# GpSimd passes in pieces of 256 columns, and one exponential per head for the decay matrix

## Chip, cores and metric

The kernel runs on one core of a Trainium2 chip. The metric is device time in microseconds (us) of one execution; the time before is the median of three runs.

## What is computed

One layer of an encoder over two requests (4096 and 2048 tokens of width 1024, that is 32 + 16 tiles of 128 tokens) with shared weights. The input is layer-normalised, projected, split among three mixers (windowed attention, a gated DeltaNet in both directions, attention over 256 memory tokens), gated, projected out, added to the input and normalised again. The parts that the change touches:

```python
def layer_norm(x, g, b):                      # on the input and on the memory tokens
    mu = xf.mean(-1, keepdims=True); var = jnp.square(xf - mu).mean(-1, keepdims=True)
    return (xf - mu) * lax.rsqrt(var + LN_EPS) * g + b
...
q = l2norm(heads(q)) * DN_KEY_DIM ** -0.5     # l2norm(t) = t * rsqrt(sum(t*t) + 1e-6)
k = l2norm(heads(k))
...
g = jnp.cumsum(g, axis=-1)
decay = exp(where(causal, g[..., :, None] - g[..., None, :], -inf))
k_beta = k * beta[..., None]
a = einsum('...id,...jd->...ij', k_beta, k) * decay      # then a triangular solve with a
qk = einsum('...id,...jd->...ij', q, k) * decay
```

The kernel works with the decay matrix multiplied by the step's beta, so each of its entries is the exponential of a sum: the row of cumulated gates of the one position, less the cumulated gate of the other, plus the logarithm of beta, plus a mask that is 0 or -30000.

## The kernel before

The work stands in three stages, each over the 48 tiles in pairs. Stage one (0 to about 1390 us) makes for each tile the input norm (`front`), the projections (`proj`), the short convolution and the normalised keys and queries of the DeltaNet (`conv`), and the windowed attention (`attention`). Stage two (about 1560 to 2450 us) runs the DeltaNet forward in time, with the gates' projections (`gate_proj`) and the memory attention (`memory`) beside it; stage three (2450 us to the end) runs it backward in time, with the output projection and the last norm (`finish`) beside it. Between stages one and two both overlap.

No line of the source is issued at once. `V`, `S`, `G`, `T` and `Q` (VectorE, ScalarE, GpSimd, TensorE and the DMA queue of SyncE) are recorders of the class `Plan`: each call is noted with its tiles and a cost from a table (for GpSimd 200 ns + 2.1 ns a column). When a pool closes, a list scheduler puts all noted operations of a stage in order, engine by engine, by those costs, the number of buffers of each tile and the latest time at which each operation is due; it makes seven orders and keeps the one that its own costs like best. Its costs know of no engine that holds up another. Then everything is issued in that order, and all engines work strictly in order. So all compute instructions have the one source line L505, and are told apart by tiles.

The places that the change touches:

- `front` (L819): for each of 48 input tiles and 4 tiles of memory tokens. VectorE takes the statistics (`bst`, `bmv`), GpSimd the power -1/2 (`brs`), ScalarE normalises `x` (128x1024, f32) in place, GpSimd multiplies `x` by the row `grow` and adds the row `brow`, each in one instruction over 1024 columns. Then `split` makes a high half (ScalarE) and a low half (VectorE, `xhl`), and a DMA transposes both to `xT`. `x` has three buffers, `xhl` one, `xT` two (of a pair each).
- `conv` (L1414): for each pair of tiles, per three blocks, a convolution of five taps: ScalarE the first, VectorE four `scalar_tensor_tensor` on `acc` for each of two halves. Then per tile GpSimd adds halves to `n32` (tile `n`), ScalarE squares, VectorE sums (`nss`) and adds an epsilon, GpSimd takes the power -1/2, VectorE multiplies by 1024, GpSimd multiplies `n32` by it (512 columns), and `split` makes `kqtm`.
- `gates` (L1362): six times, for eight tiles at once, the gates: `lnb` is the logarithm of beta, `ncum` the negative cumulated gate (a copy on ScalarE from PSUM).
- `dn_prep` (L869): for each tile and direction (96 times). `e` is the tile `cr` (128 x 4 heads x 128), loaded as a broadcast row. VectorE adds the mask; ScalarE adds `ncum` for each of four heads (Identity with a bias), then takes the exponential for each head with the bias `lnb`. VectorE multiplies the two products in PSUM (`psk`) with it, to `n` and `p`.
- `dn_invert`: for each four tiles a triangular inverse on GpSimd, 60 dependent instructions (`tb`, `nb`) after two DMAs.

Of the kernel before, what the change touches and what calls it, by code (L numbers as in the profile page):

```python
# [13 lines left out]
AF = mybir.ActivationFunctionType  # L14
ALU = mybir.AluOpType
# [4 lines left out]
P = 128  # L20
D = 1024
# [529 lines left out]
def encoder(ctx: ExitStack, tc: tile.TileContext, A, outs):  # L551
    nc = tc.nc
    plan = Plan(tc)
    V, S, G, T, Q = plan.engines()
# [12 lines left out]
    def ctile(shape, dt, name):  # L567
        return const.tile(shape, dt, name=name, tag=name)
# [7 lines left out]
    def sc1(name):  # L576
        nscal[0] += 1
        return scal[:, nscal[0] - 1:nscal[0]]
# [209 lines left out]
    ncum = ctile([P, 2, NT, 4], F32, "ncum")  # L788
    lnb = ctile([P, 2, NT, 4], F32, "lnb")
# [27 lines left out]
    grow_in, brow_in = grow, brow  # L817

    def front(pool, src_rows, xT_out, hl_dram=None, x_dram=None):  # L819

        x = gx.tile([P, D], F32, tag="x", name="x", bufs=3)
        Q.dma_start(out=x, in_=src_rows)
        rs, nb = layer_norm_stats(pool, x, LN_EPS, "f")
        S.activation(x, x, AF.Identity, scale=rs, bias=nb)
        G.tensor_tensor(x, x, grow_in, op=ALU.mult)
        G.tensor_tensor(x, x, brow_in, op=ALU.add)
        hl = pool.tile([P, 2, D], F16, tag="xhl", name="xhl", bufs=1)
        split(None, hl[:, 0, :], hl[:, 1, :], x)
        flat = hl.rearrange("p a b -> p (a b)")
        if xT_out is not None:  # L830
            Q.dma_start_transpose(out=xT_out, in_=flat)
        if hl_dram is not None:
            Q.dma_start(out=hl_dram, in_=flat)
        if x_dram is not None:
            Q.dma_start(out=x_dram, in_=x)
# [33 lines left out]
    def dn_prep(pool, psp, dr, t, e, n):  # L869

        fm = pool.tile([P, 8, P], F16, tag="fm", name="fm", bufs=2)
        Q.dma_start_transpose(out=fm, in_=dst_d[t].rearrange("p h t s d -> p (h t s d)"))

        ks = pool.tile([P, 4, P], F16, tag="ks", name="ks", bufs=KSB)
        kv = fm.rearrange("p (h t) m -> p h t m", t=2)[:, :, 1]
        for i in range(2):
            S.activation(ks[64 - 64 * i:128 - 64 * i], kv[64 * i:64 * i + 64], AF.Copy)
        lb = lnb[:, dr, t]
        nc_ = ncum[:, dr, t]
        d = {}  # L880

        V.tensor_tensor(e, e, dmask[dr][2].unsqueeze(1).to_broadcast([P, 4, P]), op=ALU.add)
        for h in range(4):
            S.activation(e[:, h], e[:, h], AF.Identity, bias=nc_[:, h:h + 1])
        for h in range(4):
            S.activation(e[:, h], e[:, h], AF.Exp, bias=lb[:, h:h + 1])
        d["eg"] = egs[:, :, dr, t]

        p = pool.tile([P, 4, P], F32, tag="p", name="p", bufs=1)
        for hp in range(2):  # L890
            hs = slice(2 * hp, 2 * hp + 2)
            psk = psp.tile([P, 2, 2, P], F32, tag="fr", name="psk", bufs=1)
            for h2 in range(2):
                h = 2 * hp + h2
                T.matmul(psk[:, :, h2], lhsT=fm[:, 2 * h + 1, :], rhs=fm[:, 2 * h:2 * h + 2, :],
                         start=True, stop=False)
                T.matmul(psk[:, :, h2], lhsT=ks[:, h, :], rhs=fm[:, 2 * h:2 * h + 2, :], start=False, stop=True)
            V.tensor_tensor(n[:, hs], psk[:, 1], e[:, hs], op=ALU.mult)
            V.scalar_tensor_tensor(p[:, hs], psk[:, 0], -(2.0 ** 10), e[:, hs], op0=ALU.mult, op1=ALU.mult)
        d["n"] = n  # L900
        phl = pool.tile([P, 2, 4, P], F16, tag="phl", name="phl", bufs=2 * PAIRS)
        split(None, phl[:, 0], phl[:, 1], p)
        d["phl"] = phl
        d["t"], d["dr"] = t, dr
        return d
# [247 lines left out]
    bias = biasp.tile([P, AH, 386], F32, name="bias", tag="bias")  # L1153
# [42 lines left out]
    eps_k = sc1("eps_k")  # L1196
# [165 lines left out]
    def gates(b, pool, tags):  # L1362

        ts = slice(b * NG, min(NT, b * NG + NG))
        n = ts.stop - ts.start
        xe = pool.tile([P, 2, NG, 16], F32, tag=tags[0][0], name="gx", bufs=tags[0][1])
        w = pool.tile([P, 6, NG, 16], F32, tag=tags[1][0], name="gw", bufs=tags[1][1])[:, :, 0:n]
        x, e = xe[:, 0, 0:n], xe[:, 1, 0:n]
        Q.dma_start(out=x, in_=ab_d[b])
        z = w[:, 0]  # L1370
        V.tensor_tensor(z[:, :, 0:8], x[:, :, 0:8], dtb.unsqueeze(1).to_broadcast([P, n, 8]), op=ALU.add)
        V.tensor_scalar(z[:, :, 8:16], x[:, :, 8:16], -1.0, None, op0=ALU.mult)

        V.tensor_scalar(w[:, 1], z, -1.0, None, op0=ALU.mult)
        V.tensor_tensor(e, z, w[:, 1], op=ALU.min)
        S.activation(e, e, AF.Exp)
        V.tensor_scalar(w[:, 2], e, 2.0, None, op0=ALU.add)
        V.reciprocal(w[:, 2], w[:, 2])
        V.tensor_tensor(w[:, 3], e, w[:, 2], op=ALU.mult)
        V.tensor_tensor(w[:, 4], w[:, 3], w[:, 3], op=ALU.mult)  # L1380
        V.tensor_scalar(w[:, 5], w[:, 4], 1.0 / 15.0, None, op0=ALU.mult)
        for k in range(6, 0, -1):
            V.scalar_tensor_tensor(w[:, 5], w[:, 5], 1.0 / (2 * k + 1), w[:, 4], op0=ALU.add, op1=ALU.mult)
        V.scalar_tensor_tensor(w[:, 5], w[:, 5], 1.0, w[:, 3], op0=ALU.add, op1=ALU.mult)
        V.tensor_scalar(z, z, 0.0, None, op0=ALU.max)
        V.scalar_tensor_tensor(z, w[:, 5], 2.0, z, op0=ALU.mult, op1=ALU.add)
        V.tensor_scalar(lnb[:, :, ts], z[:, :, 8:16].rearrange("p t (d h) -> p d t h", d=2), -1.0, -LN20,
                        op0=ALU.mult, op1=ALU.add)
        g = z[:, :, 0:8]
        V.tensor_tensor(g, g, nea.unsqueeze(1).to_broadcast([P, n, 8]), op=ALU.mult)  # L1390
        V.tensor_scalar(g, g, GMIN, None, op0=ALU.max)
        gg = xe[:, 1].rearrange("p t c -> p (t c)").bitcast(F16)[:, 0:16 * n]
        gg = gg.rearrange("p (a d t h) -> p a d t h", a=2, d=2, h=4)
        gd = g.rearrange("p t (d h) -> p d t h", d=2)
        V.tensor_copy(gg[:, 0], gd)
        V.tensor_tensor(gg[:, 1], gd, gg[:, 0], op=ALU.subtract)
        ps = pj.tile([P, 512], F32, tag="pw", name="psg", bufs=1)
        ps3 = ps[:, 0:24 * n].rearrange("p (i d t h) -> p i d t h", i=3, d=2, h=4)
        pst = ps[0:4 * n, 256:512].rearrange("p (d i) -> p d i", d=2)
        for dr in range(2):  # L1400
            U, L, _ = dmask[dr]
            for i, st in enumerate((U, L, ones16)):
                for a in range(2):
                    T.matmul(ps3[:, i, dr], lhsT=st, rhs=gg[:, a, dr], start=(a == 0), stop=(a == 1))
            for a in range(2):
                T.matmul(pst[:, dr], lhsT=gg[:, a, dr], rhs=U, start=(a == 0), stop=(a == 1))
        cT = pool.tile([P, 2, P], F32, tag=tags[2][0], name="cT", bufs=tags[2][1])[0:4 * n]
        S.activation(cT, pst, AF.Copy)
        Q.dma_start(out=crow_d[b].rearrange("d t h i -> (t h) d i"), in_=cT)
        S.activation(ncum[:, :, ts], ps3[:, 0], AF.Copy, scale=-1.0)  # L1410
        V.scalar_tensor_tensor(ps3[:, 1], ps3[:, 1], LN20, lnb[:, :, ts], op0=ALU.add, op1=ALU.add)
        S.activation(egs[:, :, :, ts], ps3, AF.Exp)

    def conv(pp):  # L1414

        c = cb[pp]
        raws = []
        for f0 in (0, 2, 4):
            acc = pa.tile([P, 2, 256], F32, tag="acc", name="acc", bufs=2)
            for f in range(2):  # L1420
                S.activation(acc[:, f], c[:, f0 + f, 0:256], AF.Copy, scale=cw[:, f0 + f, 0:1])
                for j in range(1, 5):
                    V.scalar_tensor_tensor(acc[:, f], c[:, f0 + f, j:j + 256], cw[:, f0 + f, j:j + 1], acc[:, f],
                                           op0=ALU.mult, op1=ALU.add)
# [9 lines left out]
        for tb in range(2):  # L1434
            t = 2 * pp + tb
            n32 = pa.tile([P, 2, 4, 64], F32, tag="n32", name="n32", bufs=1)
            sq = pa.tile([P, 2, 4, 64], F32, tag="nsq", name="nsq", bufs=1)
            ss = pa.tile([P, 2, 8], F32, tag="nss", name="nss", bufs=2)
# [2 lines left out]
                                raws[i][:, 1, :, tb, :], op=ALU.add)  # L1441
            S.activation(sq, n32, AF.Square)
            V.tensor_reduce(ss[:, 0], sq.rearrange("p q h d -> p (q h) d"), axis=AX.X, op=ALU.add)
            V.tensor_scalar(ss[:, 0], ss[:, 0], eps_k, None, op0=ALU.add)
            G.tensor_tensor(ss[:, 1], ss[:, 0], nhalf.to_broadcast([P, 8]), op=ALU.pow)
            V.tensor_scalar(ss[:, 1], ss[:, 1], 1024.0, None, op0=ALU.mult)
            n3 = n32.rearrange("p q h d -> p (q h) d")
            G.tensor_tensor(n3, n3, ss[:, 1].unsqueeze(2).to_broadcast([P, 8, 64]), op=ALU.mult)
            kqtm = pa.tile([P, 4, 2, 2, 64], F16, tag="kqtm", name="kqtm", bufs=1)
            o = kqtm.rearrange("p h t s d -> p t h s d")  # L1450
            split(None, o[:, :, :, 0, :], o[:, :, :, 1, :], n32)
# [382 lines left out]
```

## Time and profile before

| | |
|---|---|
| median of 3 runs | 3352.14 us (3349.26 to 3354.52) |
| the profiled execution, its own time | 3363.07 us |
| its span in the trace | 3361.0 us |
| VectorE (DVE) busy | 2920.9 us, 87% of the span |
| TensorE (PE) busy | 2870.1 us, 85% |
| ScalarE (ACT) busy | 2441.2 us, 73% |
| GpSimd (POOL) busy | 1711.0 us, 51% |

The profile is of one execution. Busy time of an engine is the union of its instructions' spans: an instruction that has started and is held up is busy all the same, so a held instruction shows as a long one. The mean of a group of equal instructions against their median tells how much holding is in it. The chain of waits is followed back from the last instruction to what released each; its shares tell what the time was spent on where nothing else could have gone on.

### The profile page before, as it was taken

The page shows a single profiled execution, that of the slowest core. Times are in us where ns is not written, and L with a number is a line of the kernel's source. Part 1 is how long each engine was busy: PE and PEld are TensorE (multiplying, and loading weights), DVE is VectorE, ACT ScalarE, POOL GpSimd, SP SyncE. Part 2 cuts the span into 40 slices and gives each one's busy share as a digit, 9 for nine tenths or more (in the row PEclk, how much of TensorE's full clock was granted, in tenths as well). Part 3 has the DMA queues.
Part 4 walks back from the last instruction along what each step waited for, and adds up shares of the span by engine and source line. Part 5 has one row for each costly group of instructions (what it writes and reads, how often), then busy time and mean ns, then how long its engine had stood idle before and what let it go on. Part 6 is the DMA issues. An engine that isn't in the chain of part 4 may idle for free.

```text
span 3361.0 us, 82755 instructions
## 1 busy us (share of the span) xinstructions
PE 2870.1 (85%) x29856; PEld 1893.3 (56%) x29856; DVE 2920.9 (87%) x6850; ACT 2441.2 (73%) x6253; POOL 1711.0 (51%) x2611
## 2 busy tenths in 40 slices
PE   5788888788898887767899999999988988998988
PEld 4566666666676665444556555555554544444544
DVE  7999868799999989678889888888878988888997
ACT  4577656767777776688888878777877777777764
POOL 3644424344444334546645455455528666657662
PEclk9899998899999998878999999999998999999999
DMA  6999999999999999898678887778788777877775
GB/s 203 239 224 220 219 222 222 234 230 220 212 233 220 200 224 247 210 223 180 165 191 194 206 181 178 172 161 181 172 190 194 191 183 179 193 179 188 183 175 154
DMA packets 1336916, 671.43 MB, mean 200 GB/s; under 512 B 1127728, under 2 KB 1243312, under 8 KB 1332280
## 3 DMA queue, kind: packets, MB, share of 16 engines
q1 hardware_dynamic: 1336504, 666.14, 86.3%
q8 instruction: 234, 3.83, 0.5%
q14 instruction: 178, 1.46, 0.1%
HBM read 240.12 MB, written 181.49 MB: 125 GB/s over the span
## 4 chain that ended last, share of the span: by engine, by line
DVE 31%; PE 20%; POOL 15%; DMA 13%; issue 10%; ACT 8%; SPq 3%; POOLq 0%; ACTq 0%; DVEq 0%
POOL nb L505 5%; DVE acc L505 5%; POOL tb L505 5%; PE pso L505 5%; PE psg L505 5%; PE psf L505 3%; SPq L505 3%; DVE lg L505 3%; DVE aphl L505 3%; PE psk L505 2%; ACT lg L505 1%; PE psq L505 1%; DMA uc<-ud 1%; PE pslg L505 1%; DVE rx L505 1%
## 5 line engine op out<-in xcount | busy, mean ns | idle before, releaser
L505 PEld LDWEIGHTS <-xT 128*128 128x128 f16 x5760 | 535.5, 99 | 385.2 <-issue 52.5
L505 PE MATMUL psg<-w2a,xT 128*128 128x512 f16 (+1 forms) x2304 | 446.0, 334 | 9.6 <-DVE qtm L505 8.0
L505 PE MATMUL psf<-xT,w1f 128*128 128x256 f16 (+1 forms) x3600 | 439.9, 276 | 14.7 <-DMA xT<-xhl 6.3
L505 PEld LDWEIGHTS <-w1f 128*128 128x128 f16 x3600 | 341.7, 101 | 59.4 <-issue 10.8
L505 POOL TENSOR_TENSOR nb<-nb,tb 128x30 f32<-128x30 f32 (+6 forms) x750 | 348.6, 465 | 49.3
L505 POOL TENSOR_TENSOR tb<-nb,na 128x30 f32<-128x30 f32 (+6 forms) x750 | 342.6, 457 | 48.3
L505 ACT ACTIVATE lg<-lg,mx,scal 128x385 f32<-128x385 f32 (+1 forms) x384 | 263.8, 688 | 122.3 <-DVE mx L505 107.6
L505 PE MATMUL pslg<-kfm,qfm 128*128 128x128 f16 x2240 | 201.0, 233 | 164.1 <-DVE mx L505 149.4
L505 DVE SCALAR_TENSOR_TENSOR acc<-cb,cw,acc 128x256 f32<-128x256 f32 x576 | 329.8, 605 | 4.1 <-POOL cb L505 1.7
L505 PEld LDWEIGHTS <-qfm 128*128 128x128 f16 x2624 | 204.2, 104 | 222.3 <-issue 188.0
L505 PEld LDWEIGHTS <-yT 128*128 128x128 f16 x2304 | 200.1, 99 | 216.1 <-issue 27.7
L505 PE MATMUL pso<-w2a,yT 128*128 128x512 f16 x1152 | 311.4, 394 | 9.6 <-DMA yT<-yhl 7.1
L505 PE MATMUL pso<-w2b,yT 128*128 128x512 f16 x1152 | 298.9, 383 | 0.0
L505 PE MATMUL psg<-w2b,xT 128*128 128x512 f16 x1152 | 289.3, 382 | 3.8 <-DMA w2b<-w_d 3.8
L505 PE MATMUL psq<-w1t,xT 128*128 128x512 f16 x1152 | 287.0, 385 | 0.2 <-ACT cb L505 0.2
L505 DVE TENSOR_TENSOR aphl<-lg,aphl 128x768 f16<-128x768 f32 (+1 forms) x192 | 209.9, 1096 | 49.7 <-ACT aphl L505 49.3
L505 POOL TENSOR_TENSOR n<-raw 128x256 f32<-128x256 f16 x96 | 82.3, 867 | 262.2 <-DMA raw<-cfh 62.1
L505 DVE CUSTOM_DVE_ANT_0 lg<-pslg,bias 128x385 f32<-128x385 f32 (+1 forms) x384 | 195.3, 539 | 17.7 <-PE pslg L505 13.5
L505 POOL TENSOR_TENSOR x<-x,grow 128x1024 f32<-128x1024 f32 x52 | 128.0, 2462 | 121.8 <-ACT x L505 117.6
L505 PEld LDWEIGHTS <-th 64*64 64x64 f16 x2304 | 99.1, 111 | 131.1 <-issue 106.1
L505 PE MATMUL psk<-w1t,xT 128*128 128x272 f16 x1152 | 161.4, 287 | 13.5 <-DVE qktm L505 10.0
L505 PE MATMUL psx<-rx,th 64*64 64x64 f16 x2304 | 126.8, 197 | 41.3 <-DVE rx L505 29.8
(1026 smaller groups left out, 7607.8 us busy)
## 6 DMA issues: line engine op xcount, KB each, us to landing
x<-x SPq DMA_DIRECT2D x48, 512.0 KB, 4.3
xT<-xT SPq DMA_DIRECT2D x24, 1024.0 KB, 5.5
xT<-xT SPq DMA_DIRECT2D x48, 512.0 KB, 4.5
n<-dn SPq DMA_DIRECT2D x96, 256.0 KB, 3.3
r<-x SPq DMA_DIRECT2D x48, 512.0 KB, 4.4
out_dram<-r SPq DMA_DIRECT2D x48, 512.0 KB, 3.8
cr<-crow SPq DMA_DIRECT2D x47, 512.0 KB, 5.1
yhl<-yhl SPq DMA_DIRECT2D x48, 384.0 KB, 3.4
```

Source lines behind the costliest of these rows:

```text
L505: getattr(self.eng[o["e"]], o["name"])(*o["args"], **o["kw"])
```

## The change

Four edits.

1. `front`: GpSimd's two passes over 1024 columns become eight instructions of 256 columns, multiply and add in turn for each quarter.
2. `dn_prep`: the four Identity instructions per tile are gone; the one exponential per head has the bias `ncum`, which now holds the sum of both exponents.
3. `gates`: that sum is made where `ncum` is written: one VectorE instruction from PSUM in place of ScalarE's copy.
4. `conv`: the factor 1024 moves into the argument of the power (2^-20, in the instruction that adds the epsilon), and VectorE's multiplication after the power is gone; GpSimd's multiplication of `n32` becomes two of 256 columns.

```diff
@@ front
-        G.tensor_tensor(x, x, grow_in, op=ALU.mult)
-        G.tensor_tensor(x, x, brow_in, op=ALU.add)
+        for c in range(0, D, 256):
+            xc = x[:, c:c + 256]
+            G.tensor_tensor(xc, xc, grow_in[:, c:c + 256], op=ALU.mult)
+            G.tensor_tensor(xc, xc, brow_in[:, c:c + 256], op=ALU.add)
@@ dn_prep
-        lb = lnb[:, dr, t]
         nc_ = ncum[:, dr, t]
...
         for h in range(4):
-            S.activation(e[:, h], e[:, h], AF.Identity, bias=nc_[:, h:h + 1])
-        for h in range(4):
-            S.activation(e[:, h], e[:, h], AF.Exp, bias=lb[:, h:h + 1])
+            S.activation(e[:, h], e[:, h], AF.Exp, bias=nc_[:, h:h + 1])
@@ gates
-        S.activation(ncum[:, :, ts], ps3[:, 0], AF.Copy, scale=-1.0)
+        V.scalar_tensor_tensor(ncum[:, :, ts], ps3[:, 0], -1.0, lnb[:, :, ts], op0=ALU.mult, op1=ALU.add)
@@ conv
-            V.tensor_scalar(ss[:, 0], ss[:, 0], eps_k, None, op0=ALU.add)
+            V.tensor_scalar(ss[:, 0], ss[:, 0], eps_k, 2.0 ** -20, op0=ALU.add, op1=ALU.mult)
             G.tensor_tensor(ss[:, 1], ss[:, 0], nhalf.to_broadcast([P, 8]), op=ALU.pow)
-            V.tensor_scalar(ss[:, 1], ss[:, 1], 1024.0, None, op0=ALU.mult)
-            n3 = n32.rearrange("p q h d -> p (q h) d")
-            G.tensor_tensor(n3, n3, ss[:, 1].unsqueeze(2).to_broadcast([P, 8, 64]), op=ALU.mult)
+            for i in range(2):
+                G.tensor_tensor(n32[:, i], n32[:, i], ss[:, 1, 4 * i:4 * i + 4].unsqueeze(2).to_broadcast([P, 4, 64]),
+                                op=ALU.mult)
```

Since the planner sees other operations with other costs, it also writes the order of every engine anew. GpSimd's queue in the middle of stage one before (`x` is the input tile in `front`; `n_1551`, `n_1556`, `v_1555` are tiles of `conv`, `nss` its power, `brs` the power of the input norm):

```order
L505 TENSOR_TENSOR nss<-nss,scal 128x8
L505 TENSOR_TENSOR n_1551<-n_1551,nss 128x512
L505 TENSOR_TENSOR x<-x,grow 128x1024
L505 TENSOR_TENSOR v_1555<-raw 128x256
L505 TENSOR_TENSOR x<-x,brow 128x1024
L505 TENSOR_TENSOR brs<-bmv,scal 128x1
```

and the same place with the change:

```order
L505 TENSOR_TENSOR nss<-nss,scal 128x8
L505 TENSOR_TENSOR n_1551<-n_1551,nss 128x256 x2
L505 TENSOR_TENSOR brs<-bmv,scal 128x1
L505 TENSOR_TENSOR x<-x,grow 128x256 x2
L505 TENSOR_TENSOR x<-x,brow 128x256 x2
L505 TENSOR_TENSOR x<-x,grow 128x256 x2
L505 TENSOR_TENSOR x<-x,brow 128x256 x2
L505 TENSOR_TENSOR n_1556<-raw 128x256 x2
```

Here the eight pieces of a tile stand together; at other tiles other work stands between them, so a little further on (`n_1651` is another tile of `conv`, `cb` a copy of border columns):

```order
L505 TENSOR_TENSOR x<-x,grow 128x256 x2
L505 TENSOR_TENSOR nss<-nss,scal 128x8
L505 COPY cb<-cb 128x6x2
L505 TENSOR_TENSOR n_1651<-n_1651,nss 128x256 x2
L505 TENSOR_TENSOR x<-x,brow 128x256
L505 COPY cb<-cb 128x6x2
L505 TENSOR_TENSOR x<-x,brow 128x256
```

The power (`nss`) and what follows it now pass between pieces of one tile. ScalarE's queue where the forward DeltaNet prepares its tiles, before (`cr` with `ncum` is the Identity, `cr` with `lnb` the exponential):

```order
L505 ACTIVATE cr<-cr,ncum 128x128
L505 ACTIVATE cr<-cr,lnb 128x128 x4
L505 ACTIVATE cr<-cr,ncum 128x128 x2
L505 ACTIVATE tnh<-psg_21520,scal 128x512
L505 ACTIVATE sqw<-xw 128x512
L505 ACTIVATE cr<-cr,ncum 128x128
```

and with the change, where `cr` with `ncum` is the exponential:

```order
L505 ACTIVATE phl<-p 128x512
L505 ACTIVATE cr<-cr,ncum 128x128 x4
L505 ACTIVATE gx<-gx 128x128
L505 ACTIVATE cr<-cr,ncum 128x128 x4
L505 ACTIVATE sqw<-xw 128x512 x2
```

Of the eight instructions per tile that stood between the mask and the products, four are left.

## Rows read from the trace of the kernel before

**Rows 1.** The page: busy time (share) and instructions; the chain by engine
```profile
PE 2870.1 (85%) x29856; PEld 1893.3 (56%) x29856; DVE 2920.9 (87%) x6850; ACT 2441.2 (73%) x6253; POOL 1711.0 (51%) x2611
...
DVE 31%; PE 20%; POOL 15%; DMA 13%; issue 10%; ACT 8%; SPq 3%; POOLq 0%; ACTq 0%; DVEq 0%
```

**Rows 2.** Busy time by stage: PE, PEld, DVE, ACT, POOL, PEclk, DMA share, GB/s
```profile
200.00:1390.00 1190.00, 987.63 (x10730) 766.87 (x10729) 1057.49 (x2414) 832.93 (x2008) 490.80 (x396) 0.94 1.02 226
...
1560.00:2450.00 890.00, 815.97 (x8835) 508.27 (x8833) 775.82 (x1854) 712.11 (x1934) 474.52 (x943) 0.97 0.79 180
2450.00:3361.00 911.00, 804.40 (x7826) 439.21 (x7824) 792.56 (x1863) 655.72 (x1741) 543.71 (x980) 0.95 0.77 183
```

**Rows 3.** The chain by line, in 200:800 and in 800:1390
```profile
by line: issue 13.7%; DVE acc L505 12.6%; DVE lg L505 7.4%; PE psf L505 6.0%; DVE aphl L505 5.8%; SPq L505 3.9%; PE psq L505 3.5%; ACT lg L505 3.4%; DVE nss L505 2.9%; PE pslg L505 2.8%; DVE bst L505 2.6%; DMA wm<-wm_d 2.1%; PE psk L505 2.1
...
by line: DVE acc L505 14.2%; issue 14.0%; DVE lg L505 7.7%; DVE aphl L505 7.4%; PE psf L505 7.2%; DVE mx L505 3.7%; ACT lg L505 3.7%; PE psq L505 3.5%; PE pslg L505 3.0%; DVE nss L505 2.8%; PE psk L505 2.3%; SPq L505 2.1%; DVE cfh L505 2.0%
```

**Rows 4.** VectorE's groups in 200:1390: busy us, mean ns | idle before
```profile
L505 DVE SCALAR_TENSOR_TENSOR acc<-cb,cw,acc 128x256 f32<-128x256 f32 x535 | 305.0, 602 | 4.1 <-POOL cb L505 1.7 <-ACT acc L505 1.3
L505 DVE TENSOR_TENSOR aphl<-lg,aphl 128x768 f16<-128x768 f32 (+1 forms) x172 | 186.2, 1085 | 46.6 <-ACT aphl L505 46.2
...
L505 DVE TENSOR_TENSOR cfh<-acc,cfh 128x512 f16<-128x512 f32 x66 | 60.2, 913 | 19.2 <-ACT cfh L505 19.1
...
L505 DVE TENSOR_SCALAR mx<-mx,scal 128x4 f32<-128x4 f32 x85 | 38.5, 453 | 0.2
...
L505 DVE TENSOR_REDUCE nss<-nsq 128x8 f32<-128x512 f32 x43 | 29.0, 675 | 5.3 <-ACT nsq L505 5.1
...
L505 DVE TENSOR_SCALAR nss<-nss 128x8 f32<-128x8 f32 x43 | 21.3, 495 | 6.2 <-POOL nss L505 6.1
...
L505 DVE TENSOR_SCALAR nss<-nss,scal 128x8 f32<-128x8 f32 x43 | 12.6, 293 | 0.1
```

**Rows 5.** By tile, whole span: ns min/median/max, first and last start
```profile
L505 DVE SCALAR_TENSOR_TENSOR acc<-cb,cw,acc x576: 421/475/2644, 95.4 to 1386.4; 128x256 f32<-128x256 f32 x192
L505 DVE TENSOR_TENSOR cfh<-acc,cfh x72: 646/682/2843, 121.9 to 1403.9; 128x512 f16<-128x512 f32 x72
L505 DVE TENSOR_TENSOR aphl<-lg,aphl x192: 676/950/3107, 123.8 to 1427.8; 128x768 f16<-128x768 f32 x176, 128x512 f16<-128x512 f32 x16
L505 DVE TENSOR_SCALAR mx<-mx,scal x96: 196/220/2318, 120.2 to 1422.6; 128x4 f32<-128x4 f32 x96
L505 DVE TENSOR_SCALAR nss<-nss x48: 153/172/2332, 145.8 to 1427.5; 128x8 f32<-128x8 f32 x48
L505 POOL TENSOR_TENSOR x<-x,grow x52: 2342/2366/3393, 12.2 to 1273.1; 128x1024 f32<-128x1024 f32 x52
L505 POOL TENSOR_TENSOR x<-x,brow x52: 2328/2404/3211, 15.0 to 1278.3; 128x1024 f32<-128x1024 f32 x52
L505 POOL TENSOR_TENSOR yd<-of,yd x48: 719/729/1742, 2521.3 to 3338.3; 128x256 f32<-128x256 f32 x48
L505 DVE TENSOR_TENSOR kgtm<-kg,kgtm x96: 642/684/1168, 1462.0 to 3306.6; 128x512 f16<-128x512 f32 x96
```

**Rows 6.** The timeline of VectorE, then of GpSimd, 766:774: start us, us
```profile
766.18 2.25 DVE L505 TENSOR_SCALAR nss<-nss 128x8 f32<-128x8 f32 x1
...
770.35 3.55 DVE L505 SCALAR_TENSOR_TENSOR acc<-cb,cw,acc 128x256 f32<-128x256 f32 x3
...
766.04 2.36 POOL L505 TENSOR_TENSOR x<-x,grow 128x1024 f32<-128x1024 f32 x1
...
770.69 2.54 POOL L505 TENSOR_TENSOR x<-x,brow 128x1024 f32<-128x1024 f32 x1
```

**Rows 7.** VectorE's groups in 2450:3361
```profile
L505 DVE TENSOR_TENSOR kc<-kc,kc 128x512 f16<-128x512 f32 x47 | 34.6, 737 | 0.3
L505 DVE TENSOR_TENSOR kgtm<-kg,kgtm 128x512 f16<-128x512 f32 x46 | 34.2, 743 | 0.2
```

**Rows 8.** Groups over the whole span, of ScalarE and VectorE
```profile
L505 ACT ACTIVATE cr<-cr,ncum 128x128 f32<-128x128 f32 x384 | 135.9, 390 | 12.8 <-DVE cr L505 11.5
...
L505 DVE TENSOR_SCALAR nss<-nss 128x8 f32<-128x8 f32 x48 | 24.4, 509 | 12.2 <-POOL nss L505 11.9
```

## The prediction, made before the changed kernel was run

> **What bounds the kernel now.** I read the page first [rows 1]. No engine is full: VectorE 87%, TensorE 85%, ScalarE 73%, GpSimd 51%. The chain is spread in the same way, 31% on VectorE, 20% on TensorE, 15% on GpSimd, 8% on ScalarE. So no saving of busy time is worth its whole length, and what a microsecond is worth has to be read stage by stage.
>
> The stages come next [rows 2]. In stage one (200 to 1390 us) VectorE is busy 1057.49 of 1190 us, 89%; TensorE 83%, ScalarE 70%, GpSimd 41%. The chain there, in its two halves, names VectorE's convolution (`acc`) with 12.6 and 14.2%, far ahead of any TensorE group, and `aphl`, `lg` and `nss` of VectorE behind it [rows 3]. Stage one is bound by VectorE. In the later stages TensorE leads (816 of 890 and 804 of 911 us), and ScalarE is at 80 and 72%.
>
> Then the question of why VectorE is so busy in stage one. Its groups' means [rows 4] stand far over the medians of the same tiles [rows 5]: `acc` 602 against 475 ns, `aphl` 1085 against 950, `cfh` 913 against 682, `mx` 453 against 220, the multiplication of `nss` 495 against 172. The longest of each, 2318 to 3107 ns, is its median plus about 2.2 us, nearly the length of one GpSimd pass over `x` (medians 2366 and 2404 ns). The timeline shows it directly [rows 6]: GpSimd's pass runs from 766.04 for 2.36 us, and the multiplication of `nss`, normally 0.17 us, lasts from 766.18 for 2.25, to just after the pass's end. At 770.35 three `acc`, which are worth 1.4 us, take 3.55 while the second pass runs. A VectorE instruction of these kinds that starts during a GpSimd pass is held until it ends.
>
> **The change part by part.**
>
> What the holding costs now. Mean less median, times the count in 200 to 1390: `acc` 127 ns x 535 = 68 us, `aphl` 135 x 172 = 23, `cfh` 231 x 66 = 15, `mx` 233 x 85 = 20, `nss` 323 x 43 = 14. Together 140 us of VectorE's busy time.
>
> The multiplication of `nss` goes as a whole: 24.4 us busy in the whole span [rows 8], 14 of it from the 140. It was held so often because GpSimd, having finished the power, went on to the next pass in its queue before VectorE could start. After the change the power's reader is GpSimd itself. This leaves 126 us of surplus.
>
> Pieces in place of passes. One piece has the form of `yd`, 128x256, f32, both operands in SBUF: median 729 ns [rows 5]. What a VectorE instruction loses beside short GpSimd instructions is seen in stage three, where GpSimd is busier (543.71 of 911 us, 60%) but with 980 instructions of 0.55 us on average [rows 2]. There `kgtm` and `kc`, the same operation and shape as `cfh`, have means of 743 and 737 ns [rows 7] against a median of 684, and the longest `kgtm` is 1168 [rows 5]. The surplus is 59 and 53 ns, against 231 for `cfh` beside the long passes: a quarter, and a third when scaled by 0.73 / 0.55. By this row 126 us would fall to 42, a gain of 84. The other bound is that nothing is gained: as much is lost in more portions. I take half, a gain of 63, nearer to the row of the same form; I don't take the whole third, since the long passes weren't the only holders, and since the new order puts all eight pieces of many tiles in a row.
>
> What a microsecond of VectorE is worth in stage one. On the chain `acc` has 12.6% of 600 and 14.2% of 590 us, 159 us, of 305 busy: 0.52. `aphl` has 79 of 186: 0.42. `nss` has 2.9 and 2.8%, 34 us, of the 63 that its three groups are busy: 0.54 [rows 3, 4]. I take 0.5. The 63 + 24 = 87 us are worth **-43.5 us**.
>
> GpSimd gets more work: eight pieces of 0.729 us are 5.83 us per tile against 2.366 + 2.404 = 4.77, so 1.06 us x 52 = 55 us more. The halves of the multiplication of `n` add little. In stage one GpSimd has 700 us of idle time to cover it, `x` has three buffers, and no GpSimd group is among the printed lines of the chain, the last of which has 2.0% (some 12 us in each half). Without that cover all 55 us would count. I charge **+3 us**.
>
> ScalarE loses 384 Identity instructions, 135.9 us [rows 8], all in preparing DeltaNet tiles, mostly in stages two and three. ScalarE has 8% of the chain, 269 us, for 2441.2 busy [rows 1]: 0.11 for each microsecond. That gives **-15 us**. Bounds: nothing, if TensorE's work and GpSimd's inversions hide all of it; -49, if ScalarE's time were worth what VectorE's is on average (31% of 3361 over 2920.9, 0.36). What is late next in preparing a tile is then VectorE's `n` and `p`. I stay at the low value because TensorE is over 88% busy in both stages.
>
> The six copies that become VectorE instructions in `gates`, and the second operand in the epsilon's instruction, are **+0.5 us** together.
>
> The sum is -43.5 + 3 - 15 + 0.5 = -55 us. The profiled execution took 3363.07 us and would take 3308; the median of the runs is 10.9 us lower (3352.14), so the forecast is **3297 us**.
>
> **The rivals.**
>
> *Each piece holds VectorE again (slower).* Between two pieces VectorE runs the waiting instruction, GpSimd takes its turn, and VectorE's next instruction waits for a whole piece. Its place is the runs of `acc` in stage one. Were each of 416 pieces to cost VectorE its full 0.729 us, it would lose 303 us where it now loses 126, 177 more; less 24 for `nss` this is +153 x 0.5 = +77, with -15 and +3 about +65: 3417 us. It decides from the point where the loss exceeds 126 + 24 + 24 = 174 us (the last 24 being the other terms, 12 us, at 0.5), that is 0.42 us per piece. For it: the eight pieces often stand in a row, and at 770.35 VectorE is held as soon as one `acc` is through. Against it: the inversions put 60 dependent GpSimd instructions in a row, and `kgtm` beside them loses 59 ns on average. Chance 0.12.
>
> The Trainium skill's page "SBUF — State Buffer", section "🔬 SBUF: two separate sides", says that VectorE and GpSimd share a pair of ports as an exclusive lock for a whole instruction, and that a VectorE instruction with two SBUF inputs, or in a two-port mode, and a GpSimd instruction that reads SBUF block each other, the later one fully. The trace agrees, with 2.25 us where 0.17 is usual [rows 6]. By this rule cutting a pass shortens one hold but takes the lock eight times in place of two, so by itself it speaks as much for this rival as for the forecast.
>
> *VectorE's time is freed and stays idle.* TensorE is 83% busy in stage one and the DMA engines show a share of 1.02 [rows 2]; if transposes or projections end last as soon as VectorE is faster, only a tenth of the 43.5 us comes through: -4 - 15 + 3 = -16, 3336 us; without ScalarE's part it is no change. The planner's new order can have the same effect. For it: "issue" is 13.7 and 14.0% of that chain. Against it: DMA and TensorE groups there are single-digit lines. Chance 0.20.
>
> *The pieces act as one pass.* If VectorE never gets in between consecutive pieces, the holds stay as they are, or grow by 5.83 / 4.77. Then only `nss` and ScalarE count: -12 - 15 + 3 + 0.5 x 28 = -10, 3342 us. Against it: `kgtm` never exceeds 1168 ns beside 60 instructions in a row. Chance 0.05.
>
> **How the numbers follow.** The forecast has 0.63, the rivals 0.12, 0.20 and 0.05. A difference under 0.2% (6.7 us) can't be told from none. Faster: 0.63 + 0.12 of the second rival + 0.03 of the third = 0.78. Same: 0.08, from the second. Slower: 0.12 from the first and 0.02 from the third, 0.14. The best case has 84 + 24 us of VectorE at 0.54 and -49 of ScalarE: -58 - 49 + 3 = -104, 3248 us. The range is 3245 to 3355: it takes in the second and third rivals, and leaves out the first, and little below.
>
> **What would show each step.** Right: in 200 to 1390 us the mean of `acc` falls from 602 to about 535 ns and the longest to under 1.5 us; `mx` comes near 300; VectorE's busy time falls by some 90 us, and the end of stage one comes 35 to 45 us earlier; each piece takes 0.73 to 0.85 us; ScalarE is busy about 2305 us; stages two and three together are 10 to 20 us shorter. Wrong: a mean of `acc` at 600 or over means the first or third rival (the first if the longest is short, the third if it stays over 2 us); a mean that falls while VectorE's idle time grows by as much means the second; and stages two and three over 40 us shorter would mean that ScalarE was priced too low.

## The result, and the profile after

The changed kernel takes 3300.4 us (median of 4 runs, 3294.81 to 3304.61) against 3350.7 us for the kernel before on the same chip; the ratio is 0.9849, 95% interval 0.983 to 0.9869. That is 51 us or 1.5% faster, where -55 us (3297 us) was forecast. The profiled execution took 3304.61 us, its span is 3302.1 us. It lies 4 us above the median of its runs, the profiled execution of before (3363.07 us) 12 us: the two spans differ by 59 us, the runs by 51.

The page after: busy time of each engine (compare [rows 1]).

```profile
PE 2863.6 (87%) x29856; PEld 1886.9 (57%) x29856; DVE 2850.6 (86%) x6808; ACT 2335.2 (71%) x5863; POOL 1816.5 (55%) x2971
```

VectorE is busy for 70 us less (87 were forecast), ScalarE for 106 less, GpSimd for 105 more. The page's chain could be followed back for only 2% of this span, so nothing is read from it here.

The stages after (compare [rows 2]): PE, PEld, DVE, ACT, POOL, clock, DMA share, GB/s.

```profile
200.00:1344.00 1144.00, 970.64 (x10601) 750.51 (x10599) 992.46 (x2336) 822.52 (x1974) 579.49 (x670) 0.95 1.06 231
...
1500.00:2400.00 900.00, 820.05 (x8943) 514.64 (x8941) 776.88 (x1877) 672.45 (x1773) 487.01 (x958) 0.96 0.79 178
2400.00:3302.00 902.00, 801.34 (x7855) 437.42 (x7853) 791.34 (x1865) 607.59 (x1581) 532.16 (x986) 0.96 0.78 185
```

Two marks divide the span: the start of the last `acc` (end of stage one) and of the last `ofs` (end of the forward direction). By tile after (compare [rows 5]): ns min/median/max, first and last start.

```profile
L505 DVE SCALAR_TENSOR_TENSOR acc<-cb,cw,acc x576: 422/476/1755, 64.2 to 1339.4; 128x256 f32<-128x256 f32 x192
L505 DVE TENSOR_TENSOR cfh<-acc,cfh x72: 666/684/1228, 117.5 to 1352.5; 128x512 f16<-128x512 f32 x72
L505 DVE TENSOR_TENSOR aphl<-lg,aphl x192: 675/957/1536, 107.9 to 1381.1; 128x768 f16<-128x768 f32 x176, 128x512 f16<-128x512 f32 x16
L505 DVE TENSOR_SCALAR mx<-mx,scal x96: 204/222/773, 104.9 to 1377.1; 128x4 f32<-128x4 f32 x96
L505 POOL TENSOR_TENSOR x<-x,grow x208: 713/736/1775, 12.2 to 1231.4; 128x256 f32<-128x256 f32 x104
L505 POOL TENSOR_TENSOR x<-x,brow x208: 716/902/1722, 14.7 to 1233.3; 128x256 f32<-128x256 f32 x104
```

The last `acc` starts at 1339.4 us where it was 1386.4: stage one is 47 us shorter, and what follows it 12 us. Those 12 us are not all gain: by the runs 51 less 47, some 4 us, are left for what follows stage one. The run f3_decay_old_order (below), which has the instructions of before in the same order up to 1346 us, shows how far one execution can be read: its last `acc` starts at 1386.3 us (in the middle of stage one the two are up to 8 us apart), its span is 9 us shorter, and by the runs it is no faster. The longest of the held instructions have come down from 2.3 to 3.1 us to 0.8 to 1.8 us, with the medians where they were. The 1755 ns are of one `acc`, at 1330.7 us, which waited through a copy and both halves of `n` on GpSimd; beside pieces of `x` alone no `acc` takes over 1040 ns.

VectorE's groups after, 200 to 1343 us (compare [rows 4]): busy, mean ns | idle before.

```profile
L505 DVE SCALAR_TENSOR_TENSOR acc<-cb,cw,acc 128x256 f32<-128x256 f32 x528 | 285.3, 571 | 4.0 <-POOL cb L505 2.5
L505 DVE TENSOR_TENSOR aphl<-lg,aphl 128x768 f16<-128x768 f32 (+1 forms) x171 | 180.1, 1056 | 43.7 <-ACT aphl L505 43.3
...
L505 DVE TENSOR_TENSOR cfh<-acc,cfh 128x512 f16<-128x512 f32 x66 | 52.8, 800 | 3.1 <-ACT cfh L505 2.9
...
L505 DVE TENSOR_SCALAR mx<-mx,scal 128x4 f32<-128x4 f32 x85 | 27.7, 326 | 0.3
```

The surplus of mean over median, by the prediction's reckoning, is 95 ns x 528 = 50 us, 99 x 171 = 17, 116 x 66 = 8 and 104 x 85 = 9: 84 us in place of 126. More instructions are held, and each for less: counted in the two traces, 80 of the 576 `acc` took over 700 ns before, 1415 on average; after, 134, 899 on average. GpSimd's own side has two rows, over the whole span:

```profile
L505 POOL TENSOR_TENSOR x<-x,brow 128x256 f32<-128x256 f32 x208 | 193.0, 944 | 0.0
L505 POOL TENSOR_TENSOR x<-x,grow 128x256 f32<-128x256 f32 x208 | 185.5, 908 | 122.0 <-ACT x L505 110.7 <-issue 6.9 <-DVE grow L505 4.5
```

A piece takes 0.93 us on average where 0.73 is its undisturbed length. The timeline shows why, first VectorE, then GpSimd:

```profile
750.36 2.77 DVE L505 SCALAR_TENSOR_TENSOR acc<-cb,cw,acc 128x256 f32<-128x256 f32 x3
...
750.38 1.61 POOL L505 TENSOR_TENSOR x<-x,grow 128x256 f32<-128x256 f32 x2
751.94 1.77 POOL L505 TENSOR_TENSOR x<-x,brow 128x256 f32<-128x256 f32 x2
```

Three `acc` worth 1.4 us and four pieces worth 2.9 us run side by side over 3.4 us. Each `acc` takes about 0.92 us, twice its length, and three of the four pieces are longer than usual as well: here the two engines take turns. What the pieces bought is that a turn is short.

### The profile page after: what moved, and what is told of

Same layout as the page of the kernel before. It is cut to its first block, busy times and chain, and to the rows that moved or that the text cites. A ratio compares the mean times of both kernels' runs of the same rounds, so it can differ in the third digit from the quotient of the medians.

```text
span 3302.1 us, 82658 instructions
## 1 busy us (share of the span) xinstructions
PE 2863.6 (87%) x29856; PEld 1886.9 (57%) x29856; DVE 2850.6 (86%) x6808; ACT 2335.2 (71%) x5863; POOL 1816.5 (55%) x2971
## 5 line engine op out<-in xcount | busy, mean ns | idle before, releaser
L505 DVE SCALAR_TENSOR_TENSOR acc<-cb,cw,acc 128x256 f32<-128x256 f32 x576 | 313.5, 575 | 5.8 <-POOL cb L505 4.0
L505 POOL TENSOR_TENSOR x<-x,grow 128x256 f32<-128x256 f32 x208 | 185.5, 908 | 122.0 <-ACT x L505 110.7
L505 DVE TENSOR_TENSOR aphl<-lg,aphl 128x768 f16<-128x768 f32 (+1 forms) x192 | 201.1, 1050 | 55.0 <-ACT aphl L505 54.5
L505 POOL TENSOR_TENSOR x<-x,brow 128x256 f32<-128x256 f32 x208 | 193.0, 944 | 0.0
L505 PE MATMUL psov<-vtm,apt 128*128 128x64 f16 x3360 | 136.6, 197 | 53.4 <-DMA apt<-aphl 52.9
(1024 smaller groups left out, 7411.8 us busy)
```

Of the source, the lines that this page charges most:

```text
L505: getattr(self.eng[o["e"]], o["name"])(*o["args"], **o["kw"])
```

## The experiments

All twelve compare with the kernel before on the same chip, by the ratio of runs; the sets ran on different chips (the median of before was 3350.7 to 3358.8 us from set to set), so differences below are ratios turned into us with the set's own median. The marks are those of the one profiled execution, which lies between 3 us below and 12 us above the median of its runs; differences of marks under some 10 us are not shown by them.

| run | ratio to before | us | last `acc` | last `ofs` | span |
|---|---|---|---|---|---|
| before | | | 1386.4 | 2500.3 | 3361.0 |
| the change | 0.9849 [0.983, 0.9869] | -51 | 1339.4 | 2448.0 | 3302.1 |
| e1_pieces_alone | 0.9906 [0.9888, 0.9924] | -32 | 1360.1 | 2461.0 | 3316.5 |
| e2_conv_alone | 1.0056 [1.0039, 1.0074] | +19 | 1403.8 | 2513.9 | 3370.2 |
| e3_decay_alone | 1.0039 [1.0024, 1.0055] | +13 | 1405.8 | 2511.1 | 3364.6 |
| e7_before_replanned | 1.0058 [1.0045, 1.0071] | +19 | 1404.7 | 2507.8 | 3371.7 |
| f1_pieces_old_order | 0.9899 [0.9883, 0.9915] | -34 | 1356.8 | 2469.2 | 3326.9 |
| f2_conv_old_order | 0.9979 [0.9969, 0.9989] | -7 | 1375.9 | 2486.1 | 3347.4 |
| f3_decay_old_order | 1.0001 [0.9989, 1.0013] | 0 | 1386.3 | 2494.6 | 3352.3 |
| f4_all_old_order | 0.9893 [0.9875, 0.991] | -36 | 1350.0 | 2462.8 | 3324.1 |
| g1_passes_new_order | 0.9982 [0.9972, 0.9992] | -6 | 1385.1 | 2492.3 | 3346.7 |
| g2_identity_new_order | 0.9901 [0.9888, 0.9915] | -33 | 1342.4 | 2462.9 | 3326.3 |
| h1_pieces128_new_order | 0.9882 [0.9861, 0.9904] | -40 | 1358.0 | 2464.2 | 3319.9 |
| e8_after_replanned | 0.9864 [0.9847, 0.9881] | -46 | 1349.7 | 2448.2 | 3313.7 |

### Each edit alone, re-planned

The theory: the three parts add up as in the prediction's sum, and it is the work and the holding that count. The rivals: the gain of stage one is that of the edit in `conv`; or the new order alone makes it.

The pieces alone:

```diff
-        G.tensor_tensor(x, x, grow_in, op=ALU.mult)
-        G.tensor_tensor(x, x, brow_in, op=ALU.add)
+        for c in range(0, D, 256):
+            xc = x[:, c:c + 256]
+            G.tensor_tensor(xc, xc, grow_in[:, c:c + 256], op=ALU.mult)
+            G.tensor_tensor(xc, xc, brow_in[:, c:c + 256], op=ALU.add)
```

> The kernel before with the first edit alone: eight GpSimd pieces of 256 columns per tile in place of two passes of 1024. My theory (a VectorE instruction is held for the rest of the GpSimd instruction that it meets, so shorter instructions hold it for less): about -28 us (63 us of VectorE at 0.5, less 3 for GpSimd), all of it in stage one; the mean of acc falls from 602 to about 535 ns, its longest to under 1.8 us. Rival A (each piece holds VectorE again; the gain of stage one came from the edit in conv): within 8 us of before or slower, mean of acc at 600. Rival B (the planner's new order made the difference): any value, and the three edits apart don't add up to the 50 us that they give together.

Measured -32 us; the longest `acc` 1268 ns, its mean 579. The time and the longest are as the theory has it, the mean is not (535 was expected), and the run without any edit, below, shows that a re-planned kernel proves little by itself.

The edit in `conv` alone:

```diff
-            V.tensor_scalar(ss[:, 0], ss[:, 0], eps_k, None, op0=ALU.add)
+            V.tensor_scalar(ss[:, 0], ss[:, 0], eps_k, 2.0 ** -20, op0=ALU.add, op1=ALU.mult)
...
-            V.tensor_scalar(ss[:, 1], ss[:, 1], 1024.0, None, op0=ALU.mult)
-            n3 = n32.rearrange("p q h d -> p (q h) d")
-            G.tensor_tensor(n3, n3, ss[:, 1].unsqueeze(2).to_broadcast([P, 8, 64]), op=ALU.mult)
+            for i in range(2):
+                G.tensor_tensor(n32[:, i], n32[:, i], ss[:, 1, 4 * i:4 * i + 4].unsqueeze(2).to_broadcast([P, 4, 64]),
+                                op=ALU.mult)
```

> The kernel before with the edit in conv alone: the factor 1024 in the power's argument, VectorE's multiplication of nss gone, GpSimd's multiplication of n in two halves. My theory: 24.4 us of VectorE at 0.5 go, -12 us, all in stage one; the means of acc and mx stay near 600 and 450 ns, since the passes still hold. Rival A (the gain of stage one came from this edit): -35 us or more. Rival B (the new order): any value.

Measured +19 us: work was taken away, and the kernel became slower. The merged exponential alone:

```diff
-            S.activation(e[:, h], e[:, h], AF.Identity, bias=nc_[:, h:h + 1])
-        for h in range(4):
-            S.activation(e[:, h], e[:, h], AF.Exp, bias=lb[:, h:h + 1])
+            S.activation(e[:, h], e[:, h], AF.Exp, bias=nc_[:, h:h + 1])
...
-        S.activation(ncum[:, :, ts], ps3[:, 0], AF.Copy, scale=-1.0)
+        V.scalar_tensor_tensor(ncum[:, :, ts], ps3[:, 0], -1.0, lnb[:, :, ts], op0=ALU.mult, op1=ALU.add)
```

> The kernel before with the merged exponential alone (the edits in dn_prep and gates). My theory: 136 us of ScalarE at 0.11, -15 us, none of it in stage one, whose end stays within 5 us of before. Rival C (ScalarE's time is hidden wholly): 0, within 5 us. Rival D (ScalarE was worth as much as VectorE): -40 us or more.

Measured +13 us, although this edit hardly touches stage one, which ended 19 us later. And none of the edits, another order:

```diff
-    LAT = {"PE": 200.0, "DVE": 150.0, "ACT": 170.0, "POOL": 40.0, "SP": 0.0}
+    LAT = {"PE": 200.0, "DVE": 155.0, "ACT": 170.0, "POOL": 40.0, "SP": 0.0}
```

> The kernel before with none of the edits; only the planner's figure for what VectorE's results take to be seen is 155 in place of 150 ns, so that the same instructions are put in another order on every engine. My theory (the work and the holding count, not the order): within 10 us of before. Rival B (the order alone makes differences of the size seen): 20 us or more away, either way.

Measured +19 us. My theory (within 10 us) is wrong here, and rival B (20 us or more) is right but for 1 us: with the same instructions an order can be 19 us worse. All three re-planned kernels that keep the long passes end stage one at 1404 to 1406 us. The order of the kernel before was better for stage one than these three, by some 18 us, and single edits that are re-planned can't be read for effects of this size.

### Each edit alone, in an order that is kept

So the next kernels give the planner exactly what the kernel before gives it, and replace instructions only when they are issued; an operation can carry a function that is called at its place:

```diff
                 for i in self.order():
                     o = self.ops[i]
+                    if "alt" in o:
+                        o["alt"]()
+                        continue
                     getattr(self.eng[o["e"]], o["name"])(*o["args"], **o["kw"])
...
+    def issue(fn):
+        plan.ops[-1]["alt"] = fn
```

For the pieces:

```diff
         G.tensor_tensor(x, x, grow_in, op=ALU.mult)
+        issue(lambda: [nc.gpsimd.tensor_tensor(x[:, c:c + 256], x[:, c:c + 256], grow_in[:, c:c + 256], op=ALU.mult)
+                       for c in range(0, D, 256)])
         G.tensor_tensor(x, x, brow_in, op=ALU.add)
+        issue(lambda: [nc.gpsimd.tensor_tensor(x[:, c:c + 256], x[:, c:c + 256], brow_in[:, c:c + 256], op=ALU.add)
+                       for c in range(0, D, 256)])
```

> The first edit alone in the order of before: the planner is given the two passes, and when it issues them each is replaced by four pieces of 256 columns at the same place; all other queues are the same, row by row. My theory (shorter holds): -28 us, between -15 and -45, all in stage one. Rival A (each piece holds again): within 8 us or slower. Rival B (the pieces gain only through the new order that they bring): within 8 us of before.

Measured -34 us (29 to 39). In its trace the queues of VectorE, ScalarE and TensorE hold the instructions of before in the same order. Its `acc` by tile:

```profile
L508 DVE SCALAR_TENSOR_TENSOR acc<-cb,cw,acc x576: 423/475/1341, 95.6 to 1356.8; 128x256 f32<-128x256 f32 x192
```

and its page, busy times:

```profile
PE 2862.5 (86%) x29856; PEld 1885.2 (57%) x29856; DVE 2866.0 (86%) x6850; ACT 2445.5 (74%) x6253; POOL 1801.1 (54%) x2923
```

With every queue in its old order, and GpSimd's passes cut in four, the longest `acc` falls from 2644 to 1341 ns (that one beside an instruction of 512 columns on `n`; beside pieces of `x` alone it is 1046), VectorE's busy time by 55 us, and stage one ends 30 us earlier. This settles the main mechanism: how long VectorE is held follows from the length of GpSimd's instruction. 30 of 55 us is 0.54 us for each that VectorE is freed.

Which groups were freed, over the whole span, before:

```profile
L505 DVE SCALAR_TENSOR_TENSOR acc<-cb,cw,acc 128x256 f32<-128x256 f32 x576 | 329.8, 605 | 4.1 <-POOL cb L505 1.7 <-ACT acc L505 1.3
...
L505 DVE TENSOR_TENSOR aphl<-lg,aphl 128x768 f16<-128x768 f32 (+1 forms) x192 | 209.9, 1096 | 49.7 <-ACT aphl L505 49.3
...
L505 DVE TENSOR_TENSOR cfh<-acc,cfh 128x512 f16<-128x512 f32 x72 | 64.8, 899 | 19.2 <-ACT cfh L505 19.1
```

and in this run:

```profile
L508 DVE SCALAR_TENSOR_TENSOR acc<-cb,cw,acc 128x256 f32<-128x256 f32 x576 | 316.1, 581 | 10.0 <-POOL cb L508 8.5 <-ACT acc L508 0.6
...
L508 DVE TENSOR_TENSOR aphl<-lg,aphl 128x768 f16<-128x768 f32 (+1 forms) x192 | 196.5, 1026 | 44.6 <-ACT aphl L508 44.4
...
L508 DVE TENSOR_TENSOR cfh<-acc,cfh 128x512 f16<-128x512 f32 x72 | 57.7, 801 | 20.0 <-ACT cfh L508 20.0
```

`mx` goes from 42.0 to 33.7 us, so the four groups of the prediction's 126 us lose 42.5; the multiplication of `nss`, which this kernel still has, goes from 24.4 [rows 8] to 14.5, 9.9 less.

The edit in `conv`: VectorE's multiplication gets `issue(lambda: None)`, the instruction before it gets the second operand, GpSimd's multiplication two halves.

> The edit in conv alone in the order of before: VectorE's multiplication of nss is not issued, the factor stands in the power's argument, GpSimd's multiplication of n is two instructions at its place. My theory: -12 us, so that the +20 us of the re-planned version were its order. Rival E (the edit itself costs time, since the halves or the shorter wait set free something that collides): +10 us or more here too.

Measured -7 us (4 to 10): 23 us of VectorE gone (2897.5 busy), GpSimd 20 us busier (1730.6), stage one 10.5 us shorter by the marks. Rival E falls; the +19 of the re-planned version was its order.

The merged exponential: the Identity instructions get `issue(lambda: None)`, each exponential the bias `ncum`, the copy in `gates` VectorE's instruction.

> The merged exponential alone in the order of before: the Identity instructions are not issued, the sum in gates is made by VectorE at the place of ScalarE's copy. My theory: -15 us, all behind stage one, so that the +13 us of the re-planned version were its order. Rival C (ScalarE's time is hidden): within 5 us. Rival D: -40 us or more.

Measured 0 (-4 to +4). ScalarE is busy for 108 us less, and nothing else on its page moves:

```profile
PE 2866.2 (86%) x29856; PEld 1890.6 (56%) x29856; DVE 2921.2 (87%) x6856; ACT 2332.9 (70%) x5863; POOL 1704.5 (51%) x2611
```

Rival C is right in this order. All of it together:

> All four edits in the order of before, nothing re-planned. My theory, with the parts of the prediction: -55 us, 3298; if the parts are as sized and the changed kernel's own order is neither better nor worse than that of before, it equals the changed kernel (3300) within 10 us. Rival B (part of the gain came with the new order): between before and 3325. If instead the order of before is the better one, as three re-planned versions with the long passes suggest (stage one ended 17 to 20 us later in each), this beats the changed kernel by 10 to 20 us.

Measured -36 us (30 to 42), near the -41 of its parts, and 15 us short of the changed kernel, which has the same instructions. The -55 us of my theory are not reached; it is rival B. So 36 of the 51 us are work, and 15 (6 to 24, by the two intervals) came with the order that was planned for it.

### Parts undone in the order of the changed kernel

The passes back, at the places of the first and the last piece:

```diff
             G.tensor_tensor(xc, xc, grow_in[:, c:c + 256], op=ALU.mult)
+            issue((lambda: nc.gpsimd.tensor_tensor(x, x, grow_in, op=ALU.mult)) if c == 0 else lambda: None)
             G.tensor_tensor(xc, xc, brow_in[:, c:c + 256], op=ALU.add)
+            issue((lambda: nc.gpsimd.tensor_tensor(x, x, brow_in, op=ALU.add)) if c == D - 256 else lambda: None)
```

> The changed kernel in its own order, but with the two passes of 1024 columns back: the multiplication is issued at the place of a tile's first piece, the addition at the place of its last, the six others are not issued. My theory (the holding costs, in any order): +34 us on the changed kernel, as the pieces gave in the order of before, so about 3334; longest acc over 2.3 us again. Rival F (the order that was planned for pieces suffers more, or less, from passes): over +50, or under +15.

Measured 0.9982 of before, about +45 us on the changed kernel, all in stage one: the last `acc` starts 46 us later, and what follows is as long as in the changed kernel (1962 us from there to the end, against 1963). That lies between my theory (+34) and rival F (over +50).

Its `acc` by tile:

```profile
L508 DVE SCALAR_TENSOR_TENSOR acc<-cb,cw,acc x576: 421/475/2606, 66.5 to 1385.1; 128x256 f32<-128x256 f32 x192
```

as a group over the whole span:

```profile
L508 DVE SCALAR_TENSOR_TENSOR acc<-cb,cw,acc 128x256 f32<-128x256 f32 x576 | 347.4, 633 | 5.5 <-ACT acc L508 2.3 <-POOL cb L508 1.4
```

and its busy times:

```profile
PE 2870.2 (86%) x29856; PEld 1893.7 (57%) x29856; DVE 2912.3 (87%) x6808; ACT 2335.0 (70%) x5863; POOL 1713.2 (51%) x2659
```

The long holds are back, and VectorE is busy for 62 us more (2912.3). The pieces are worth 34 us in the one order and 45 in the other: in this order the passes hold `acc` more (mean 633 ns, against 605 in the kernel before). The planner's costs know of no holding, so this difference isn't a thing it aimed at.

The Identity back in ScalarE's queue, without its bias, and each just ahead of its exponential, where the kernel before issued a tile's four first:

```diff
+            issue(lambda h=h: [nc.scalar.activation(e[:, h], e[:, h], AF.Identity),
+                               nc.scalar.activation(e[:, h], e[:, h], AF.Exp, bias=nc_[:, h:h + 1])])
```

> The changed kernel in its own order, with 384 Identity instructions of ScalarE back, each just ahead of its exponential. My theory after the runs in the old order, where their removal gave nothing: within 5 us of the changed kernel, so about 3300, and the 13 us by which the changed kernel's later stages are shorter are its order. Rival G (the new order makes use of the shorter ScalarE work): +10 us or more, about 3313, all behind stage one.

Measured 0.9901, about +17 us on the changed kernel (its interval and that of the changed kernel are just apart), nearly all of it behind stage one: the last `acc` starts 3 us later, the span ends 24 us later (its profiled execution took 7 us more than the median of its runs). My expectation is wrong, rival G is right: in an order that was planned without them, 384 instructions more are felt; in an order that had slots for them, leaving them out isn't. ScalarE's group that came back:

```profile
L893 ACT ACTIVATE cr<-cr 128x128 f32<-128x128 f32 x384 | 113.6, 296 | 10.4 <-DVE cr L508 9.5
```

It is 114 us, about what the edit took from ScalarE (106).

### Shorter pieces, and another order for the changed kernel

```diff
             G.tensor_tensor(xc, xc, grow_in[:, c:c + 256], op=ALU.mult)
+            issue(lambda c=c: [nc.gpsimd.tensor_tensor(x[:, a:a + 128], x[:, a:a + 128], grow_in[:, a:a + 128], op=ALU.mult)
+                               for a in (c, c + 128)])
```

and the same for the addition.

> The changed kernel in its own order, each piece of 256 columns issued as two of 128 at its place. My theory: a piece of 128 takes some 0.45 us (128x120 of the inversions: 0.41), 16 of them 7.2 us per tile in place of 5.8; holds get shorter again, but the same sum of GpSimd time is offered to VectorE; the mean of acc falls from 571 to about 545 ns, worth -5 us, so 3290 to 3300. Rival A (each piece holds again, so that more pieces lose more): +5 to +15 us.

Measured 0.9882; the interval overlaps that of the changed kernel by a little, so 11 us slower is likely and not certain. It isn't faster, although VectorE's holding did get smaller: busy 2811.9 us, 39 less. GpSimd pays for it (groups of 0 to 1361 us), and the next step waits:

```profile
L835 POOL TENSOR_TENSOR x<-x,grow 128x128 f32<-128x128 f32 x416 | 244.8, 616 | 129.6 <-ACT x L508 116.8 <-issue 8.2 <-DVE grow L508 4.6
L838 POOL TENSOR_TENSOR x<-x,brow 128x128 f32<-128x128 f32 x416 | 230.0, 581 | 0.0
```

Sixteen pieces of 0.60 us are 9.6 us per tile against 7.4 for eight. ScalarE's conversion of `x` (`xhl`) waits for GpSimd; longest waits in total in stage one, of this kernel (200 to 1361 us):

```profile
ACT xhl L508 <- POOL x L838: 44.0, 21, 5.5
```

and of the changed kernel (200 to 1343 us):

```profile
ACT xhl L505 <- POOL x L505: 13.9, 10, 3.0
```

The size is that of rival A, the cause isn't: the holds did not add up. The waits that grew point to GpSimd's own pace instead; no run isolates it.

The changed kernel with the planner's 150 made 155:

> The changed kernel re-planned with 155 in place of 150 ns for VectorE: the same instructions in another order. My theory (an order is worth up to 20 us either way, as with the kernel before): between 3285 and 3325, and not the same as the changed kernel within 3 us. Rival (orders for short GpSimd instructions are all alike): within 5 us of it.

Measured 0.9864, within the interval of the changed kernel. With one more order, the choice between the two expectations stays open: stage one is 10 us longer, the rest 1 us.

None of the kernels beat the changed one.

## Why the prediction was right, and where its sum was not

**Stage one is bound by VectorE, and GpSimd's passes hold it up.** Right, and shown in both orders by f1_pieces_old_order and g1_passes_new_order, where only the length and the number of GpSimd's instructions on `x` differ. VectorE is not the only bound, though: in h1_pieces128_new_order it was busy for 39 us less, and stage one did not get shorter.

**The pieces.** Forecast: 63 us of VectorE at 0.5, -31.5, and +3 for GpSimd, -28.5. Measured in the old order: -34 by the runs. The time was near, the size was not. The choice of "half" of the surplus was too much: the four groups of the 126 us lost 42.5 us in f1_pieces_old_order, and 43 in the changed kernel, a third, which is why the mean of `acc` fell to 571 and not to 535 ns. What made up for it in f1_pieces_old_order is mostly the hold of `nss`, 9.9 us, which the sum has in another term; so VectorE was freed of 55 us, at 0.54. The price of 0.5 held in the old order (0.45 in f2_conv_old_order, by the marks); in the order of the changed kernel it was 46 us for 62, 0.74.

**GpSimd's cost.** Each piece takes 0.93 us and not 0.73 to 0.85, since it waits for VectorE in turn: GpSimd is busy for 105 us more (90 with the pieces alone), not 55. No run has the charge of 3 us by itself; with the gain of the pieces at the forecast or above it, it can't have been far too low. With 128 columns the pieces were no faster, and the waits for GpSimd grew.

**The multiplication of `nss`.** Forecast -12 us, measured -7 (4 to 10): VectorE lost the time that was forecast (23 of 24 us), but the two halves, of which the prediction said that they "add little", made GpSimd 20 us busier. Whether that is what took the rest is open.

**The merged exponential.** Forecast -15 us from a price of 0.11. This is the step that failed as argued: in the order of before it gave nothing (-4 to +4), the prediction's lower bound. The 12 us by which the spans differ behind stage one look like the forecast, but by the runs only some 4 are left there, and with an order that was planned anew. Whether planning with the shorter work gains anything is not settled: putting the Identity back costs 17 us, but that shows only that the new order has no room for it.

**The order.** The prediction had it only as a way in which the second rival could come true. It is worth some 15 us of the 51, and in e7_before_replanned another order of the same instructions cost 19. That the forecast (-55) and the result (-51) agree so closely is therefore in part chance: -41 of parts and -15 of order met a sum of -55 that had no term for the order.

**The signs.** Those of the wrong cases did not come. Of the right ones, the end of stage one (47 us earlier, where 35 to 45 were named) and `mx` (326 ns, near 300) came as named or nearly so; the later stages are 12 us shorter by the marks, where 10 to 20 were named, but only some 4 by the runs. Missed were the mean of `acc` (571 for 535 ns), its longest (1755 ns, where under 1500 was named, though not beside pieces of `x`), VectorE's busy time (70 us less for 90), the length of a piece (0.93 for 0.73 to 0.85 us) and ScalarE's busy time (2335 for 2305 us).

**The rivals.** That each piece would hold VectorE again by its full length, so that more is lost than before, did not happen, though the turn-taking that it named is there at 750 us. The rule of the Trainium skill's page "SBUF — State Buffer", section "🔬 SBUF: two separate sides" (an exclusive lock for a whole instruction, the other blocks fully), agrees with both timelines. What decided, at 750 us, is that the one that waits comes next, so that an `acc` loses at most one piece; the `acc` of 1755 ns shows that this does not hold beside every run of GpSimd instructions. The second rival appeared in another place than named: not TensorE or the DMA, but in f3_decay_old_order ScalarE's freed time, 108 us, brought nothing. The third, pieces that act as one pass, is excluded by the longest `acc` beside them, 1040 ns.

## What to carry to other kernels

When an engine that is nearly full shows means far above medians, look in the timeline for the instruction of another engine that ends where the long ones end; cutting that into pieces can pay (here with 256 columns; 128 were no faster than 256, and the next step waited longer for the cut engine). In a kernel whose order a planner writes, first measure a re-plan without any edit, and compare edits in an order that is kept: here three re-planned kernels of the same or less work were 13 to 19 us slower than the one they started from. Time that is freed on an engine while the order is kept can be worth nothing: here 108 us of ScalarE were. And one profiled execution can't tell differences of some 10 us; the runs can.

## What was not expected of the hardware

- Taking turns: at 750 us `acc` instructions in a row and GpSimd's pieces of 0.73 us in a row run alternately, and both get longer (`acc` 0.92 us for 0.48, three of the four pieces to about 0.9; over the whole span a piece takes 0.93 us on average). At 1330.7 us one `acc` waited through two halves of `n` (0.60 us each), so turns are not kept everywhere.
- GpSimd's multiplication of two f32 operands takes 2.37 us for 1024 columns, 0.74 for 256 and 0.46 for 128 (medians; the last from h1_pieces128_new_order). From the first two, an estimate is 0.19 us per instruction and 2.1 ns per column, which gives 0.46 for the third.
- Taking away 384 ScalarE instructions of 390 ns, 135.9 us by their row [rows 8], lowered its busy time by 106 us only (108 in f3_decay_old_order). In the trace of before two neighbours of 0.39 us (at 2357.32 and 2357.61 us) start 0.29 us apart. The Trainium skill's page "ScalarE: Activation LUTs", section "What ACT_TABLE_LOAD costs", says that ScalarE instructions in a row overlap by about 93 ns, and the trace agrees; by that an estimate is 384 x 297 ns = 114 us, near the measured value.
